# Attention with half-row second score passes, two parts of the product with v and both transposes per unit, in a written order

## The chip, the cores and the metric

One core of one Trainium2 chip runs the whole kernel. The metric is the device time of one execution in microseconds (us). The kernel's engines are TensorE (PE; PEld is its weight load), VectorE (DVE), ScalarE (ACT), GpSimd (POOL) and SyncE (SP), which issues most DMAs. SBUF is the on-chip memory, PSUM the eight banks that TensorE writes.

## The reference

One encoder layer on 2048 tokens of width 1024: an RMS norm, an input projection, differential attention beside a retention, an output projection, and a two-layer MLP with squared ReLU. The change concerns the attention. It has 4 heads; each has two components c of queries and keys of 64 features, and values of 128:

```
s = einsum('bhcqd,bhckd->bhcqk', q_blk, k) * dk ** -0.5
p = softmax(s - slope[h] * |qpos - kpos|, axis=-1)
a = p[:, :, 0] - lam[h] * p[:, :, 1]
out = einsum('bhqk,bhkd->bhqd', a, v)
```

## The kernel before, in words

All large products run in the type fp32r on operands that are split into a high and a low part, so that a product is three matmuls (high by high, high by low, low by high; `mm3`). The stages are: input projection (to about 661 us), retention, attention (about 775 to 1363 us), output projection, MLP.

A tile is 128 queries of one head: 4 heads by 16 tiles are 64 tiles, numbered i. Two tiles are a group (256 queries). Keys of a head lie in `ka` as 128 rows by 2 components by 2048 keys; for both components rows 0 to 63 hold the high parts of the 64 features and rows 64 to 127 the low parts. `qa` holds the high parts of the queries in both halves of its rows, `qb` the low parts in both halves. So one matmul of 128 rows with `qa` gives high by high plus high by low, and a second one with `qb` (the second pass) gives low by high plus low by low.

Steps of a tile, with their lines:

- `scores` (L992): a slot is one component and half of the keys (1024). Four matmuls of 512 columns fill two PSUM banks (L1011 with `qa`, L1012 with `qb`). VectorE reads both banks in one instruction, adds the bias, writes `p` and keeps a running minimum `nm` (L1016). After a component's second half ScalarE takes the exp of 128x2048 in place and sums it into `l` (L1028). Scores have two PSUM buffers of two banks (`ps_s`).
- `combine` (L1031): VectorE computes `ratio` = -lam * l0 / l1 (L1037, L1038) and `rl` = 1 / l0 (L1039); GpSimd computes p0 += ratio * p1 in two halves, a multiplication and an addition each (L1043, L1044).
- `turn` (L1197): four transposes of p0 through TensorE (L1205) into one PSUM bank `pa` (two buffers, `ps_t`); ScalarE copies the high part `aTh` (L55), VectorE subtracts to get the low part `aTl` (L56). Four turns cover a tile's 2048 keys.
- `weigh` (L1210): the product with v, for a group: a slot is two key blocks, 6 matmuls of 256 columns (L36, L37, L38) into `po`. After the eighth slot ScalarE copies `po` to `oT` (L1223).
- `turn_back` (L1226): two transposes of `oT` (L1231), scaling by `rl` on ScalarE (L1234), and a DMA to DRAM.

The loop over i from 2 to 63 has four slots. In each slot it writes, in this order, scores of tile i, one turn of tile i - 2, one weigh slot of tile i - 4, in slot 1 of an even tile a turn_back, and after slot 3 the combination of tile i. Only TensorE follows that written order (L1239); the order on VectorE, ScalarE, GpSimd and SyncE comes from a planner that places what it expects to be ready. Tiles 0 and 1 are scored earlier, in eight steps between those of the retention (`lead_scores`, L1049, with single banks), where TensorE, VectorE and ScalarE follow the written order. `load_group` (L962) brings queries by 4 DMAs a group, `load_keys` (L940) keys by 4 DMAs a head, `load_values` (L948) the values, and computes the next head's bias from the one before on VectorE (L958). After the loop the last turns and products are interleaved with the start of the output projection.

The `p` tiles have six places, two per tile, so tile i + 3 takes the places of tile i.

Of the kernel before, what the change touches and what calls it, by code (L numbers as in the profile page):

```python
# [17 lines left out]
P = 128  # L18
# [536 lines left out]
def encoder(ctx: ExitStack, tc: tile.TileContext, a: dict, out: bass.AP, dbg=None):  # L555
# [406 lines left out]
    def load_group(g):  # L962
        h, qs = g // (S // QG), g % (S // QG) * QG
        qa = kp_.tile([P, 2, QG], F32R, tag="qa", name="qa")
        qb = kp_.tile([P, 2, QG], F32R, tag="qb", name="qb")
        for t, s in ((qa, qh_d), (qb, ql_d)):
            for half in range(2):
                d = nc.sync.dma_start(
                    t[half * 64 : half * 64 + 64].bitcast(F32),
                    s[h][:, qs : qs + QG].rearrange("(c d) q -> d c q", d=64).bitcast(F32),  # L970
                )
        groups[g] = dict(loaded=d, q=(qa, qb), a=[None] * 4, rl=kp_.tile([P, 2], F32, tag="rl", name="rl", bufs=6), po=None)
# [19 lines left out]
    def scores(i, slot, banks):  # L992

        c, hf = divmod(slot, 2)
# [4 lines left out]
        if slot == 0:  # L999
            tiles[i] = dict(p=[], l=[])  # L1000
        if hf == 0:
            tiles[i]["p"].append(hp.next([P, S], F32, "p"))
            tiles[i]["nm"] = kp_.tile([P, 4], F32, tag="nm", name="nm", bufs=8)
        p, nm = tiles[i]["p"][c], tiles[i]["nm"]
        ql = slice(qi * P, qi * P + P)
        w = 1024 // len(banks)
        for b, sc in enumerate(banks):
# [5 lines left out]
            n = hf * len(banks) + b  # L1013
            k0 = hf * 1024 + b * w
            b0 = k0 + S - P - qt * P
# [10 lines left out]
        if hf == 1:  # L1026
            l = kp_.tile([P, 1], F32, tag="l", name="l", bufs=12)
            nc.scalar.activation(p[:], p[:], AF.Exp, bias=nm[:, n : n + 1], scale=-1.0, accum_out=l[:])  # L1028
            tiles[i]["l"].append(l)

    def combine(i):  # L1031
# [4 lines left out]
        ratio = kp_.tile([P, 1], F32, tag="ratio", name="ratio", bufs=6)  # L1036
        nc.vector.reciprocal(ratio[:], ls_[1][:])  # L1037
        nc.vector.tensor_scalar(ratio[:], ratio[:], ls_[0][:], nlam[:, h : h + 1], op0=ALU.mult, op1=ALU.mult)  # L1038
        nc.vector.reciprocal(groups[g]["rl"][:, qi : qi + 1], ls_[0][:])  # L1039
# [9 lines left out]
    def lead_scores(n):  # L1049
        i, slot = divmod(n, 4)  # L1050
        scores(i, slot, [ret.bank([P, 512], "sc") for _ in range(2)])
        if slot == 3:
            combine(i)
# [136 lines left out]
    with ExitStack() as ph:  # L1190
# [6 lines left out]
        def turn(i, k4):  # L1197
            g, qi = divmod(i, 2)
            p0 = tiles[i]["p"][0]
            if qi == 0:  # L1200
# [9 lines left out]
        def weigh(g, slot):  # L1210
# [10 lines left out]
            if slot == 7:  # L1221
                oT = ap2.tile([P, QG], F32, tag="oT", name="oT")
                nc.scalar.activation(oT[:], po[:], AF.Copy)  # L1223
                groups[g]["oT"] = oT
# [14 lines left out]
        ph.enter_context(tc.manual_schedule(engines={mybir.EngineType.PE}))  # L1239
        load_values(0)  # L1240
        for i in range(LT, NI):
            for slot in range(4):
# [14 lines left out]
                if 0 < j and j % 2 == 0 and slot == 1:  # L1257
                    turn_back(j // 2 - 1)
                if slot == 3 and LEAD <= i < NI - 1:
                    combine(i)  # L1260
# [18 lines left out]
        def ws(*slots):  # L1279
            for slot in slots:  # L1280
                weigh(g - 1 + slot // 8, slot % 8)

        places = (hp.next([P, 2, DM], F32R, "wo") for _ in range(6))
        parts = [norms(tt, eg[:, 2], eg[:, 2]) for tt in (0, 4)]
        turn(NI - 2, 0)
# [5 lines left out]
        ph.enter_context(tc.manual_schedule(engines=ENGINES))  # L1291
# [340 lines left out]
```

## Time and profile before

| | |
|---|---|
| median of 3 runs | 2812.51 us (2811.05 to 2817.38) |
| profiled execution | 2811.03 us, span 2809.2 us |
| mean granted TensorE clock | 0.984 of full speed |
| attention loop, tiles 4 to 63 | 819.0 to 1341.5 us |

A profile page gives per engine the busy time and its share of the span; the chain of waits follows the work that ended last backwards, from each instruction to what released it. A line names a line of the kernel; lines 36 to 38, 50, 55 and 56 are those of helpers that several stages use. Durations of matmuls are those of one pass through the pipeline; the step from one to the next is shorter and is seen in the chain, where each piece lasts until the next begins.

### The profile page before, as it was taken

The numbers are of one execution on the slowest core, as the hardware profiler recorded it, in microseconds if no ns is written. First come the engines' busy times: TensorE is split into PE (matmuls) and PEld (weight loads), VectorE is DVE, ScalarE is ACT, GpSimd is POOL, SyncE is SP. The second block draws the span as 40 slices with busy tenths as digits, with TensorE's granted clock in tenths as the row PEclk, the third lists the DMA queues.
The fourth block names the chain that finished last, engine by engine and source line by source line (L and its number), as shares of the span: only waits on it lengthen the run. The fifth ranks groups of instructions, "written<-read, shape, count | busy, mean of one in ns | idle before, by whom it ended". The sixth has DMA issues, their size and how long they took to land.

```text
span 2809.2 us, 41043 instructions
## 1 busy us (share of the span) xinstructions
PE 2711.6 (97%) x15488; PEld 2327.6 (83%) x15488; DVE 1902.3 (68%) x2887; ACT 1303.7 (46%) x1852; POOL 1317.3 (47%) x756
## 2 busy tenths in 40 slices
PE   6998999998889999999899999999999999999999
PEld 4898989997768888888787788888888888888887
DVE  7888864787779989999898465665556435435542
ACT  5344422344457777777543345544445332222221
POOL 4235322513358787888544367765565204323320
PEclk8999999999899999999999999999999999999999
DMA  3565683259523131321367777776445848755461
GB/s 128 178 198 173 222 296 113 91 171 265 136 76 91 50 88 53 84 97 55 133 213 237 274 226 253 235 276 234 157 143 188 291 161 311 274 189 174 159 246 45
DMA packets 356518, 490.31 MB, mean 175 GB/s; under 512 B 23008, under 2 KB 252896, under 8 KB 348384
## 3 DMA queue, kind: packets, MB, share of 16 engines
q1 hardware_dynamic: 334096, 462.52, 50.4%
q10 hardware_dynamic: 21648, 20.98, 2.2%
q0 software_dynamic: 576, 4.19, 0.4%
q8 instruction: 122, 2.00, 0.3%
q14 instruction: 76, 0.62, 0.1%
HBM read 313.55 MB, written 174.06 MB: 174 GB/s over the span
## 4 chain that ended last, share of the span: by engine, by line
PE 78%; DVE 7%; DMA 2%; issue 1%; POOL 1%; ACT 1%; SPq 0%; DVEq 0%; ACTq 0%; POOLq 0%
PE ps L38 10%; PE ps L36 10%; PE ps L37 10%; PE p L36 7%; PE p L38 7%; PE p L37 7%; PE pa L1205 4%; PE sc L1011 4%; PE sc L1012 4%; PE po L36 2%; PE po L38 2%; PE po L37 2%; PE mm L38 1%; PE mm L37 1%; PE mm L36 1%
## 5 line engine op out<-in xcount | busy, mean ns | idle before, releaser
L37 PE MATMUL p<-wl,ah 128*128 128x512 f32 x896 | 348.5, 389 | 0.0
L36 PE MATMUL p<-wh,ah 128*128 128x512 f32 x896 | 348.4, 389 | 0.0
L262 POOL TENSOR_TENSOR s<-raw 128x1024 f32<-128x1024 f32 x58 | 148.0, 2552 | 373.8 <-DMA raw<-in_w_in 109.7
L303 DVE TENSOR_TENSOR c<-ps,c 128x512 f32<-128x512 f32 x360 | 238.3, 684 | 116.4 <-PE ps L38 112.1
L50 DVE TENSOR_TENSOR wl<-s,wh 128x1024 fp32r<-128x1024 f32 x120 | 192.4, 1605 | 172.0 <-ACT wh L44 172.0
L44 ACT ACTIVATE ah<-ra 128x1024 fp32r<-128x1024 f32 x112 | 112.6, 1052 | 412.6 <-PE p L37 410.8
L1044 POOL TENSOR_TENSOR p<-p 128x1024 f32<-128x1024 f32 x127 | 303.2, 2410 | 0.1
L1028 ACT ACTIVATE p<-p,nm 128x2048 f32<-128x2048 f32 x128 | 256.9, 2007 | 36.4 <-DVE nm L1016 35.4
L50 DVE TENSOR_TENSOR ah<-ra,ah 128x1024 fp32r<-128x1024 f32 x76 | 103.7, 1399 | 218.4 <-ACT ah L44 218.4
L1455 POOL TENSOR_TENSOR c<-c 128x512 f32<-128x512 f32 x128 | 196.4, 1559 | 109.5 <-ACT c L1458 107.6
L38 PE MATMUL p<-wh,ah 128*128 128x512 f32 x608 | 236.5, 389 | 0.0
L1516 POOL TENSOR_TENSOR t<-br 128x1024 f32<-128x1024 f32 x32 | 77.1, 2411 | 336.3 <-DMA br<-in_w_mlp 173.1
L44 ACT ACTIVATE wh<-s 128x1024 fp32r<-128x1024 f32 x120 | 126.5, 1057 | 208.8 <-PE ps L37 108.3
L1011 PE MATMUL sc<-ka,qa 128*128 128x512 f32 x512 | 207.1, 404 | 3.3 <-ACT yt L544 2.8
L1043 POOL TENSOR_SCALAR p<-p,ratio 128x1024 f32<-128x1024 f32 x127 | 141.8, 1129 | 143.0 <-DVE ratio L1038 111.3
L1012 PE MATMUL sc<-ka,qb 128*128 128x512 f32 x512 | 202.5, 396 | 0.0
L36 PEld LDWEIGHTS p<-wh,ah 128*128 128x128 f32 x896 | 168.2, 188 | 34.9
L37 PEld LDWEIGHTS p<-wl,ah 128*128 128x128 f32 x896 | 168.2, 188 | 34.9
L55 ACT ACTIVATE aTh<-pa 128x512 fp32r<-128x512 f32 x256 | 151.0, 591 | 82.7 <-PE pa L1205 80.1
L1016 DVE CUSTOM_DVE_ANT_0 p<-sc,bias,nm 128x1024 f32<-128x1024 f32 (+1 forms) x136 | 167.7, 1233 | 22.5 <-PE sc L1012 20.8
L1205 PEld LDWEIGHTS pa<-ident,p 128*128 128x128 f32 x1024 | 120.5, 141 | 64.9 <-issue 30.7
L56 DVE TENSOR_TENSOR aTl<-pa,aTh 128x512 fp32r<-128x512 f32 x256 | 170.2, 685 | 4.5 <-DMA vh<-vhd 3.7
(371 smaller groups left out, 8110.7 us busy)
## 6 DMA issues: line engine op xcount, KB each, us to landing
br<-in_w_mlp SPq DMA_DIRECT2D x88, 512.0 KB, 5.6
raw<-in_w_mlp SPq DMA_DIRECT2D x32, 1024.0 KB, 6.0
raw<-in_w_in SPq DMA_DIRECT2D x28, 1024.0 KB, 5.9
xt<-in_x SPq DMA_DIRECT2D x20, 512.0 KB, 5.0
q<-rqd SPq DMA_DIRECT2D x16, 512.0 KB, 10.2
qa<-qhd SPq DMA_DIRECT2D x64, 128.0 KB, 3.0
qb<-qld SPq DMA_DIRECT2D x64, 128.0 KB, 3.0
ua11d<-c SPq DMA_DIRECT2D x32, 256.0 KB, 3.0
```

Of the source, the lines that this page charges most:

```text
L36: nc.tensor.matmul(out, ah, bh, start=first, stop=False)
L37: nc.tensor.matmul(out, ah, bl, start=False, stop=False)
L38: nc.tensor.matmul(out, al, bh, start=False, stop=last)
L44: nc.scalar.activation(hi, src, AF.Copy)
L50: e.tensor_tensor(out=lo, in0=src, in1=hi.bitcast(F32), op=ALU.subtract)
L303: nc.vector.tensor_tensor(out=o[:], in0=x0[:], in1=x1[:], op=op)
L1011: nc.tensor.matmul(sc[:, o : o + 512], qa[:, c, ql], r, start=True, stop=False)
L1012: nc.tensor.matmul(sc[:, o : o + 512], qb[:, c, ql], r, start=False, stop=True)
L1028: nc.scalar.activation(p[:], p[:], AF.Exp, bias=nm[:, n : n + 1], scale=-1.0, accum_out=l[:])
L1044: e.tensor_tensor(out=p0, in0=p0, in1=p1, op=ALU.add)
L1205: nc.tensor.transpose(pa[:, j], p0[:, kt * P : (kt + 1) * P], ident[:])
L1455: nc.gpsimd.tensor_tensor(out=u[n][:], in0=u[x0][:], in1=u[x1][:], op=op)
```

## The change

- `load_keys`: component 1 of `ka` is stored with its halves exchanged, high parts in rows 64 to 127, low parts in rows 0 to 63.
- `load_group`: `qb` holds the low parts of component 0 in rows 0 to 63 and of component 1 in rows 64 to 127 (one DMA in place of two).
- `scores` works on a unit: both components, and as many keys as a buffer holds (1024 in the loop, 512 in the lead). Full passes of 128 rows with `qa` come first, then half-row passes of 64 rows with `qb` against the high parts of the keys, the two components one behind the other; low by low is no longer computed. Two reductions on VectorE follow.
- `exps` and `inverse` are functions of their own; the multiplication of `ratio` moves from VectorE to GpSimd, `rl` from `combine` to `turn`, the copy `oT` from `weigh` to `away`.
- The loop: slot 0 and slot 2 hold a unit and a weigh slot, slots 1 and 3 a weigh slot and two turns of tile i - 2. The exp of component 1 comes in slot 3 of loop i, its inverse after the first unit of loop i + 1, the exp of component 0 and the combination in slot 1 of loop i + 1.
- In the loop all four engines TensorE, VectorE, ScalarE and GpSimd follow the written order, and so they do in the part behind it.

```diff
     def load_keys(h):
...
-            rs = slice(c * 64, c * 64 + 64)
-            d = nc.sync.dma_start(ka[0:64, c].bitcast(F32), kh_d[h][rs, :].bitcast(F32))
-            nc.sync.dma_start(ka[64:128, c].bitcast(F32), kl_d[h][rs, :].bitcast(F32))
+            rs, os = slice(c * 64, c * 64 + 64), slice(64 - c * 64, 128 - c * 64)
+            nc.sync.dma_start(ka[rs, c].bitcast(F32), kh_d[h][rs, :].bitcast(F32))
+            nc.sync.dma_start(ka[os, c].bitcast(F32), kl_d[h][rs, :].bitcast(F32))
...
     def load_group(g):
...
+        nc.sync.dma_start(qb[:, 0].bitcast(F32), ql_d[h][:, qs : qs + QG].bitcast(F32))
...
-    def scores(i, slot, banks):
+    def scores(i, n, banks):
...
+        w = banks[0].shape[1]
+        k0 = n * w
+        for c, sc in enumerate(banks):
             for o in range(0, w, 512):
-                k0 = hf * 1024 + b * w + o
-                r = ka[:, c, k0 : k0 + 512]
-                nc.tensor.matmul(sc[:, o : o + 512], qa[:, c, ql], r, start=True, stop=False)
-                nc.tensor.matmul(sc[:, o : o + 512], qb[:, c, ql], r, start=False, stop=True)
+                nc.tensor.matmul(sc[:, o : o + 512], qa[:, c, ql], ka[:, c, k0 + o : k0 + o + 512], start=True, stop=False)
+        for o in range(0, w, 512):
+            for c, sc in enumerate(banks):
+                rs = slice(c * 64, c * 64 + 64)
+                nc.tensor.matmul(sc[:, o : o + 512], qb[rs, 0, ql], ka[rs, c, k0 + o : k0 + o + 512], start=False, stop=True)
...
+    def exps(i, c):
+        l = kp_.tile([P, 1], F32, tag="l", name="l", bufs=12)
+        p, n = tiles[i]["p"][c], tiles[i]["n"]
+        nc.scalar.activation(p[:], p[:], AF.Exp, bias=tiles[i]["nm"][c][:, n : n + 1], scale=-1.0, accum_out=l[:])
+        tiles[i]["l"][c] = l
+    def inverse(i):
+        tiles[i]["r"] = kp_.tile([P, 1], F32, tag="ratio", name="ratio", bufs=6)
+        nc.vector.reciprocal(tiles[i]["r"][:], tiles[i]["l"][1][:])
...
-        nc.vector.tensor_scalar(ratio[:], ratio[:], ls_[0][:], nlam[:, h : h + 1], op0=ALU.mult, op1=ALU.mult)
-        nc.vector.reciprocal(groups[g]["rl"][:, qi : qi + 1], ls_[0][:])
+        nc.gpsimd.tensor_scalar(ratio[:], ratio[:], ls_[0][:], nlam[:, h : h + 1], op0=ALU.mult, op1=ALU.mult)
...
-        ph.enter_context(tc.manual_schedule(engines={mybir.EngineType.PE}))
+        ph.enter_context(tc.manual_schedule(engines=ENGINES | {mybir.EngineType.Pool}))
...
-                if i >= LEAD:
-                    scores(i, slot, [ps_s.tile([P, 1024], F32, tag="sc", name="sc")])
-                if 0 <= i - LT:
-                    turn(i - LT, slot)
+                if slot % 2 == 0:
+                    scores(i, slot // 2, [ps_s.tile([P, 1024], F32, tag="sc", name="sc") for _ in range(2)])
+                    if slot == 0 and i > LEAD:
+                        inverse(i - 1)
                 j = i - LV
+                if 0 < j and j % 2 == 0 and slot == 0:
+                    turn_back(j // 2 - 1)
                 if 0 <= j:
                     weigh(j // 2, j % 2 * 4 + slot)
...
+                if slot % 2 == 0:
+                    continue
+                if 0 <= j and j % 2 and slot == 3:
+                    away(j // 2)
+                turn(i - LT, slot - 1)
+                turn(i - LT, slot)
+                if slot == 3:
+                    exps(i, 1)
+                elif i > LEAD:
+                    exps(i - 1, 0)
+                    combine(i - 1)
...
         parts = [norms(tt, eg[:, 2], eg[:, 2]) for tt in (0, 4)]
+        exps(NI - 1, 0)
+        inverse(NI - 1)
         turn(NI - 2, 0)
         turn(NI - 2, 1)
```

## Rows read from the trace of the kernel before

**Rows 1.** The page, busy time, share of the span and instructions of each engine.
```profile
PE 2711.6 (97%) x15488; PEld 2327.6 (83%) x15488; DVE 1902.3 (68%) x2887; ACT 1303.7 (46%) x1852; POOL 1317.3 (47%) x756
```
**Rows 2.** Busy time by stretches: stretch and length, then each engine's.
```profile
799.00:819.00 20.00, 13.93 (x65) 10.40 (x66) 14.57 (x32) 12.63 (x18) 11.28 (x8) 0.91 0.48 138
819.00:1341.50 522.50, 519.75 (x3419) 444.85 (x3418) 472.73 (x904) 404.87 (x568) 419.73 (x242) 1.00 0.26 73
```
**Rows 3.** Chain of waits in the loop: start us, length us, what.
```profile
1003.36 0.23 PE sc L1011
1003.83 0.63 PE pa L1205 x4
1004.46 0.12 PE po L36
1006.11 0.44 PE pa L1205 x4
```
**Rows 4.** Waits in the loop, 830 to 1330 us: total, times, longest.
```profile
PEld pa L1205 <- issue: 23.1, 57, 0.4
```
**Rows 5.** Chain of waits where lead scores stand between the retention's steps.
```profile
780.74 0.23 PE sc L1012
780.97 1.09 PE rS L501 x16
782.06 0.58 PE rt L542 x4
783.80 0.43 PE sc L1011
785.96 0.43 PE sc L1011
```
**Rows 6.** TensorE in order of time: start us, us, what.
```profile
780.90 1.16 PE L501 MATMUL rS<-q,kT 64*128 64x128 f32 x16
781.99 0.65 PE L542 MATMUL rt<-ident,yT 128*128 128x128 f32 x4
```
**Rows 7.** The score tiles' instructions in the loop: duration ns min/median/max.
```profile
L1012 PEld LDWEIGHTS sc<-ka,qb x480: 187/188/192, 818.8 to 1339.9; 128*128 128x128 f32 x160
L1012 PE MATMUL sc<-ka,qb x480: 387/395/398, 819.1 to 1340.1; 128*128 128x512 f32 x160
```
**Rows 8.** Groups of VectorE instructions, 830 to 1330 us: busy us, mean ns.
```profile
L1038 DVE TENSOR_SCALAR ratio<-ratio,l,nlam 128x1 f32<-128x1 f32 x58 | 15.8, 273 | 2.1
L958 DVE TENSOR_SCALAR bias<-bias 128x3968 f16<-128x3968 f16 x2 | 2.6, 1294 | 0.0
```
**Rows 9.** Groups of GpSimd instructions, in the loop and of the whole span.
```profile
L1044 POOL TENSOR_TENSOR p<-p 128x1024 f32<-128x1024 f32 x116 | 276.4, 2406 | 0.0
L1043 POOL TENSOR_SCALAR p<-p,ratio 128x1024 f32<-128x1024 f32 x116 | 129.1, 1126 | 100.7 <-DVE ratio L1038 100.7
L661 POOL IOTA prow<- 128x1 f32 x1 | 0.1, 132 | 0.0
```
**Rows 10.** One tile in order of time: transposes to copy, exp to its sum.
```profile
1101.96 0.60 PE L1205 MATMUL pa<-ident,p 128*128 128x128 f32 x4
...
1102.60 0.60 ACT L55 ACTIVATE aTh<-pa 128x512 fp32r<-128x512 f32 x1 [0.79 <-PE pa L1205]
...
1104.05 2.01 ACT L1028 ACTIVATE p<-p,nm 128x2048 f32<-128x2048 f32 x1
...
1106.18 0.16 DVE L1039 RECIPROCAL rl<-l 128x1 f32<-128x1 f32 x1 [0.48 <-ACT p L1028]
```
**Rows 11.** TensorE after the last score pass.
```profile
1342.74 0.65 PE L1205 MATMUL pa<-ident,p 128*128 128x128 f32 x4 [0.64 <-DVE aTl L56]
```
**Rows 12.** GpSimd and VectorE after the loop, in order of time.
```profile
1345.39 1.61 POOL L1043 TENSOR_SCALAR p<-p,ratio 128x1024 f32<-128x1024 f32 x1 [2.23 <-DVE ratio L1038]
1347.08 3.23 POOL L1044 TENSOR_TENSOR p<-p 128x1024 f32<-128x1024 f32 x1
1349.30 1.05 DVE L1149 TENSOR_SCALAR mst<-mst 128x4 f32<-128x4 f32 x1
```

More of the change, by code (lines that the diff above doesn't have):

```diff
@@ L965, in load_group @@
         qb = kp_.tile([P, 2, QG], F32R, tag="qb", name="qb")
[L966 to L971, printed above, removed]
+        nc.sync.dma_start(qb[:, 0].bitcast(F32), ql_d[h][:, qs : qs + QG].bitcast(F32))
+        for half in range(2):
+            d = nc.sync.dma_start(
+                qa[half * 64 : half * 64 + 64].bitcast(F32),
+                qh_d[h][:, qs : qs + QG].rearrange("(c d) q -> d c q", d=64).bitcast(F32),
+            )
         groups[g] = dict(loaded=d, q=(qa, qb), a=[None] * 4, rl=kp_.tile([P, 2], F32, tag="rl", name="rl", bufs=6), po=None)
@@ L998, in scores @@
         qa, qb = groups[g]["q"]
[L999 to L1004, printed above, removed]
+        if n == 0:
+            tiles[i] = dict(
+                p=[hp.next([P, S], F32, "p") for _ in range(2)], l={},
+                nm=[kp_.tile([P, 4], F32, tag="nm", name="nm", bufs=8) for _ in range(2)],
+            )
         ql = slice(qi * P, qi * P + P)
-        w = 1024 // len(banks)
-        for b, sc in enumerate(banks):
+        w = banks[0].shape[1]
+        k0 = n * w
+        for c, sc in enumerate(banks):
             for o in range(0, w, 512):
-                k0 = hf * 1024 + b * w + o
-                r = ka[:, c, k0 : k0 + 512]
-                nc.tensor.matmul(sc[:, o : o + 512], qa[:, c, ql], r, start=True, stop=False)
-                nc.tensor.matmul(sc[:, o : o + 512], qb[:, c, ql], r, start=False, stop=True)
-            n = hf * len(banks) + b
-            k0 = hf * 1024 + b * w
-            b0 = k0 + S - P - qt * P
+                nc.tensor.matmul(sc[:, o : o + 512], qa[:, c, ql], ka[:, c, k0 + o : k0 + o + 512], start=True, stop=False)
[3 more added lines that the diff above has]
+                nc.tensor.matmul(sc[:, o : o + 512], qb[rs, 0, ql], ka[rs, c, k0 + o : k0 + o + 512], start=False, stop=True)
+        b0 = k0 + S - P - qt * P
+        for c, sc in enumerate(banks):
+            p, nm = tiles[i]["p"][c], tiles[i]["nm"][c]
             nc.vector.tensor_tensor_reduce(
@@ L1025, in scores @@
             )
[L1026 to L1029, printed above, removed]
+        tiles[i]["n"] = n
+    def exps(i, c):
[6 more added lines that the diff above has]
+        nc.vector.reciprocal(tiles[i]["r"][:], tiles[i]["l"][1][:])
     def combine(i):
@@ L1035, in combine @@
         ps_, ls_ = tiles[i]["p"], tiles[i]["l"]
-        ratio = kp_.tile([P, 1], F32, tag="ratio", name="ratio", bufs=6)
-        nc.vector.reciprocal(ratio[:], ls_[1][:])
-        nc.vector.tensor_scalar(ratio[:], ratio[:], ls_[0][:], nlam[:, h : h + 1], op0=ALU.mult, op1=ALU.mult)
-        nc.vector.reciprocal(groups[g]["rl"][:, qi : qi + 1], ls_[0][:])
+        ratio = tiles[i]["r"]
+        nc.gpsimd.tensor_scalar(ratio[:], ratio[:], ls_[0][:], nlam[:, h : h + 1], op0=ALU.mult, op1=ALU.mult)
         for k2 in range(2):
@@ L1049, in lead_scores @@
     def lead_scores(n):
-        i, slot = divmod(n, 4)
-        scores(i, slot, [ret.bank([P, 512], "sc") for _ in range(2)])
-        if slot == 3:
+        i, part = divmod(n, 4)
+        scores(i, part, [ret.bank([P, 512], "sc") for _ in range(2)])
+        if part == 3:
+            exps(i, 1)
+            inverse(i)
+            exps(i, 0)
             combine(i)
@@ L1199, in turn @@
             p0 = tiles[i]["p"][0]
+            if k4 == 0:
+                nc.vector.reciprocal(groups[g]["rl"][:, qi : qi + 1], tiles[i]["l"][0][:])
             if qi == 0:
@@ L1220, in weigh, with away @@
                 mm3(nc, po[:], vh[:, kt], vl[:, kt], th[:, j], tl[:, j], kt == 0, kt == NT - 1)
[L1221 to L1224, printed above, removed]
+        def away(g):
+            oT = ap2.tile([P, QG], F32, tag="oT", name="oT")
+            nc.scalar.activation(oT[:], groups[g]["po"][:], AF.Copy)
+            groups[g]["oT"] = oT
         def turn_back(g):
@@ L1249, in encoder @@
                     load_group(i // 2)
[L1250 to L1253 removed]
+                if slot % 2 == 0:
+                    scores(i, slot // 2, [ps_s.tile([P, 1024], F32, tag="sc", name="sc") for _ in range(2)])
+                    if slot == 0 and i > LEAD:
+                        inverse(i - 1)
                 j = i - LV
+                if 0 < j and j % 2 == 0 and slot == 0:
+                    turn_back(j // 2 - 1)
                 if 0 <= j:
                     weigh(j // 2, j % 2 * 4 + slot)
[L1257 to L1260, printed above, removed]
+                if slot % 2 == 0:
[5 more added lines that the diff above has]
+                if slot == 3:
+                    exps(i, 1)
+                elif i > LEAD:
+                    exps(i - 1, 0)
+                    combine(i - 1)
             if i == NI - 4:
@@ L1281, in ws @@
                 weigh(g - 1 + slot // 8, slot % 8)
+                if slot % 8 == 7:
+                    away(g - 1 + slot // 8)
         places = (hp.next([P, 2, DM], F32R, "wo") for _ in range(6))
         parts = [norms(tt, eg[:, 2], eg[:, 2]) for tt in (0, 4)]
+        exps(NI - 1, 0)
+        inverse(NI - 1)
         turn(NI - 2, 0)
```

2 lines of the change are left out of this document (removed).

## The prediction

> **What bounds the kernel now.** I read the busy shares first, then the busy time by stretches, then the chain of waits, then who waits for whom. TensorE is busy for 97% of the span, VectorE for 68% [rows 1]; but shares are means over stages, so the stretches decide. Only the attention loop and its two ends are touched. From 819.0 to 1341.5 us the loop runs its 60 full tiles (4 to 63): 522.5 us, 8.71 us each, and there TensorE is busy 99.5%, VectorE 90%, GpSimd 80%, ScalarE 77% [rows 2]. Divided by 60: VectorE 7.88, GpSimd 7.00, ScalarE 6.75 us a tile. So TensorE is the bound, and the next engine is only 0.8 us behind it.
>
> The chain of waits there holds TensorE alone [rows 3]: a score pass of 512 columns steps on by 0.23 us, a pass of the product with v by 0.12, four transposes by 0.44. A tile has 16 score passes (3.73), 24 product passes (2.86), 16 transposes (1.76) and every second tile two more for the result (0.11): 8.46 us. The other 0.25 is waiting; it shows where four transposes take 0.63 instead of 0.44 [rows 3], behind the slot of the transposes' own bank (the rows give "issue", 23.1 us in 57 times [rows 4]).
>
> **The change on TensorE.** Each score unit (1024 keys, both components) had 8 full passes; it now has 4 full ones and 4 half-row ones, in two pairs, rows 0 to 63 beside rows 64 to 127. Do two halves share a step? The loop shows none, but the retention stage has such pairs: 16 passes of 64 rows and 128 columns take 1.09 us in the chain [rows 5], and from the first start to the rows' next form 1.09 again (780.90 to 781.99 [rows 6]). Alone, transposes of 128 columns step by 0.11, so 16 in a row would be 1.76. They do run in pairs. I take one score step per pair, 0.24; both bounds follow from the same rows: 0.23 (free partner) and 0.47 (no sharing).
>
> But the same rows show what it costs to go into and out of such a form. Eight pairs at 0.11 are 0.88; 1.09 is 0.21 more: the way in. On the way out, the four transposes behind them take 0.58 against the 0.44 of a group that comes straight after score passes, 0.14 more; and a full score pass straight behind half-form passes of the retention takes 0.43, twice (783.80 and 785.96), against 0.23: 0.20 more [rows 3, 5]. In and out together 0.35 to 0.41; I take 0.38. A unit goes in and out once, a tile twice: 0.76 us. The bounds: nothing (a 512-column pass, longer than the retention's, might cover the weight load; the 0.43 of a full score pass speaks against that, and no crossing in the rows is free), and 0.70 per round trip, if both crossings expose what a pass lasts beyond its step (395 - 233 ns) and a whole weight load (188 ns) [rows 7]. I stay with 0.38, since it comes from score passes themselves.
>
> Sum for TensorE: 8 full passes 1.87, 4 pairs 0.96, product 2.86, transposes 1.87 with the result's, crossings 0.76: 8.32 us against 8.46. So the halves save 0.91 and the crossings take 0.76 back.
>
> The Trainium skill has two sentences on this. TensorEngine Tiling (Array Packing), Theoretical Speedup, gives up to 2x where the contraction is 64 or less; by that alone the tile would lose 0.91 us. The same page, Key Properties, says that changing the tiling mode drains the engine; by that and the rows above it loses 0.14. The trace agrees with the second sentence (0.35 to 0.41 us a round trip), and with the first only inside a run of pairs.
>
> **The change in the order.** Transposes now come eight together, with product passes before them, and both score banks are written in one unit. What is late next, per engine, for a tile of about 8.4 us:
> - VectorE: 7.88 less the ratio's multiplication (0.27 [rows 8]), which goes to GpSimd: 7.6. The unit's second half of banks is read by the time it is wanted: from the end of a unit the two reductions take 2 x 1.2 us, and TensorE is then 12 product passes, 8 transposes and two full passes further on, 1.43 + 0.88 + 0.47 + 0.2 = 3.0.
> - ScalarE: 6.75, the same work.
> - GpSimd: 7.00 plus one small multiplication on 128x1. No row has it; VectorE's takes 0.27, GpSimd's own 128x1 iota 0.13 [rows 8, 9]. I take 0.2: 7.2.
> - A ring that did not bind before. The second exp of a tile (its component 0) now stands on ScalarE behind two copies of the tile before, these behind their transposes, these behind the combination on GpSimd, and the next combination behind that exp. Round it: first transpose to copy 0.64 (1101.96 to 1102.60), two copies 1.18, exp until its sum is there 2.13 (1104.05 to 1106.18) [rows 10], ratio 0.2, multiplication 1.13, addition of the first half 2.41 [rows 9], handshakes some 0.05: 7.74 us. Under 8.32, so it is covered, by 0.6.
>
> The waits of today (0.25) come from VectorE's splits that hold the transposes' two banks; with eight transposes once per half tile and slack on every engine most of that goes. I leave 0.08. Tile: 8.40; saved 0.31 x 60 = 18.6 us.
>
> **The ends.** (1) After tile 63 no score unit stands before the first transposes of tile 62, so the ring shows: in the loop the unit, its crossing out and 12 product passes (3.2 us) cover it; without them TensorE waits 3.2 - 0.6 = 2.6 us, where it waits 0.64 now [rows 11]: 2 us lost. (2) Three biases of later heads, 1.29 us each on VectorE [rows 8], now stand at fixed places right before the first reduction of a head. Behind each are queued two reductions, and score banks behind these; some 0.8 us of it is slack: 0.5 x 3 = 1.5 us. (3) In the lead-in both exps of a tile now come after its last quarter, 2 us later for the first; the loop's first tiles wait for other things there anyway (TensorE busy 13.9 of 20 us [rows 2]): 1 us, either sign. DMAs: a group brings 3 instead of 4, keys 4 as before, none of them among the loop's waits, of which the largest on TensorE is that of [rows 4]: nothing; without that cover a group's transfer could only come earlier, there is one less. Ends: 4.5 us lost.
>
> On (2), the Trainium skill, SBUF — State Buffer, section SBUF: two separate sides, says that VectorE in some modes and GpSimd lock each other out of a shared port for a whole instruction. A row agrees: 128x4 elements took VectorE 1.05 us and ended as GpSimd's addition did [rows 12]. By that rule a bias that meets an addition would wait up to 2.41 us more, 7 us in all, and the sum would be some 7 us later; the two biases in the loop stood where GpSimd rested.
>
> Sum: 18.6 - 4.5 = 14 us less. The profiled execution took 2811.0 us (its span is 2809.2, 1.8 us lie around it), the median of the runs is 2812.5: forecast 2798.
>
> **The rivals.**
> - *Crossings are hidden* under 512-column passes. Then TensorE needs 7.56, and the ring (7.74) is the bound; with 0.1 of waits 7.85, saved 0.86 x 60 = 52, the ends cost 6 because the ring has no slack: 2767. For it: long passes give a weight load more room. Against: the 0.43.
> - *Crossings cost more* (the slower side): place, the edges of each half-row run, four per tile; price 0.70 a round trip instead of 0.38. Tile 8.40 + 0.64 = 9.04, lost 0.33 x 60 = 20 plus 4.5: 2837. It decides from (8.71 - 8.40 + 0.76 - 0.08 for the ends) / 2 = 0.50 us a round trip on: there the loop's gain only pays for the ends. Against: no row over 0.21 a crossing.
> - *The ring binds*: GpSimd's two instructions at the 1.61 and 3.23 us of the last tile, when VectorE worked on the same kind [rows 12], give a ring of 9.0 and 2836. Against: in the loop VectorE reads banks beside it, then as now.
> - *The halves do not pair up* at this type (the pairs in the rows are of another): four more steps of 0.23, tile 9.3, 2853.
> - *Fixed order*: today's planner lets VectorE and ScalarE take what is ready; waits in line eat the 0.31: 2806 to 2818.
>
> **How the numbers follow.** Forecast 0.50 (own range 2788 to 2808), hidden 0.15, dear 0.15, ring 0.08, order 0.06, no pairs 0.06. A measurement here can tell 0.2%, 5.6 us, from no change. Faster: 0.45 + 0.15 + 0.05 from partial forms of the dear and the ordered case, 0.65; same 0.13; slower 0.22. The range takes in the hidden case and the dear bound up to 2834 and leaves out the pairless case and the tops of ring and dear, under 0.2.
>
> **What would show it.** In the profile after: pairs of half passes that start within some 10 ns of each other and step by 0.24; the full pass or product pass at either edge 0.1 to 0.2 us longer than its step, 0.76 a tile in sum; loop tiles of 8.4 us; TensorE still the bound, with VectorE at 7.6 of 8.4; a wait of 2 to 3 us for GpSimd's addition after the last score unit. A tile near 7.8 with TensorE waiting for GpSimd says that crossings are free; over 8.7 with TensorE full, that they are dear; over 8.7 with gaps, ring or order. Outside the stretch 775 to 1400 us nothing should change.

## The result, and the profile after

The changed kernel takes 2793.22 us (median of 4 runs, 2790.52 to 2793.75) against 2811.78 us (4 runs, 2810.68 to 2817.38): ratio 0.9932, 95% interval 0.9921 to 0.9944, 18.6 us less. The forecast was 2798, its own range 2788 to 2808. The profiled execution took 2790.5 us, its span 2788.7.

Busy shares of the page, in answer to [rows 1]; TensorE is still the bound. Its weight loads cover less time, not because a load of 64 rows is shorter (186 ns in the median against 188), but because the two loads of a pair run at the same time (they begin 3 to 4 ns apart, as at 1005.32):

```profile
PE 2693.0 (97%) x15488; PEld 2281.1 (82%) x15488; DVE 1884.8 (68%) x2823; ACT 1293.3 (46%) x1852; POOL 1353.8 (49%) x820
```

Busy time by stretches after the change (PE, PEld, DVE, ACT, POOL, then granted clock, DMA share, GB/s): from the first score pass to tile 4, the 60 full tiles, and the part from there to the output projection's first pass. The second line answers to the second of [rows 2]:

```profile
775.41:811.45 36.04, 30.33 (x210) 18.66 (x209) 24.85 (x60) 20.16 (x27) 15.90 (x12) 0.98 0.37 102
811.45:1315.55 504.10, 499.44 (x3418) 399.37 (x3418) 462.60 (x844) 393.95 (x568) 444.50 (x300) 1.00 0.25 68
1315.55:1340.32 24.77, 19.37 (x146) 18.05 (x143) 18.86 (x34) 18.04 (x30) 17.16 (x10) 0.93 0.04 12
```

The 60 tiles take 504.1 us where they took 522.5: 8.40 each instead of 8.71. That this is the forecast's number to the hundredth is luck: two sizes were off and cancelled (see below). By the same three stretches the trace before had 39.2, 522.5 and 21.7 us (first score pass at 779.77, the output projection's first pass at 1363.17). So the change took 3.2 us off the lead-in and 18.4 off the tiles and put 3.1 on the end: 18.5 of the 20.5 us between the two spans. (Tile 4's first pass came at 818.74 before; counted from there, 0.3 us move from the lead-in to the tiles.) The other 2 us lie in stages with the same code: the retention's first pass (L460) came at 636.07 before and 632.38 now, and between 631 and 637 in all fourteen traces of this study, so this is the spread of single executions.

The chain of waits in a unit (start, length, what), in answer to [rows 3]: no piece is late, the eight transposes take 0.87 where four took 0.63, and the product's first pass takes 0.32 behind half-row passes instead of 0.12 (the last row is the next unit's transposes):

```profile
1003.59 0.87 PE pa L1218 x8
1004.47 0.93 PE sc L1009 x4
1005.39 0.66 PE sc L1014 x4
1006.06 0.32 PE po L36
1006.38 0.12 PE po L37
...
1007.69 0.87 PE pa L1218 x8
```

The two passes of a pair begin 2 to 4 ns apart, as the prediction said of its first sign; in this row of TensorE up to 1005.33 both of the first pair have begun:

```profile
1005.32 0.50 PE L1014 MATMUL sc<-ka,qb 64*128 64x512 f32 x2
```

The second sign, a step of 0.24, does not show inside a unit: its second pair begins 0.34 us behind the first. In a longer run (**twice** below) the pairs begin 0.34, 0.57 and 0.80 us behind the first: a step of 0.23 from the second on, so the 0.1 belongs to the way in.

The waits in the loop (830 to 1310 us), TensorE's, its weight loads' and GpSimd's. The wait of the transposes' weight loads in [rows 4], 23.1 us in 57 times, is gone. The two rows of PEld are the edges of the half-row runs: before the first half-row load, and before the first full load behind them, the loads stand still for 0.36 us and wait for nothing that the profile shows.

```profile
POOL ratio L1047 <- ACT p L1033: 41.1, 54, 3.8
PEld sc L1014 <- issue: 40.8, 112, 0.4
PEld po L36 <- issue: 31.4, 86, 0.5
...
PE sc L1009 <- DVE nm L1018: 4.2, 6, 1.0
```

All of TensorE's 4.2 us lie at the three changes of head. VectorE's and GpSimd's rows there, in order of time, then TensorE's:

```profile
912.87 2.36 DVE L959 TENSOR_SCALAR bias<-bias 128x3968 f16<-128x3968 f16 x1
915.40 1.23 DVE L1018 CUSTOM_DVE_ANT_0 p<-sc,bias 128x1024 f32<-128x1024 f32 x1 [0.17 <-PE pa L1218]
```

```profile
911.78 2.40 POOL L1052 TENSOR_TENSOR p<-p 128x1024 f32<-128x1024 f32 x1
914.16 2.05 POOL L1051 TENSOR_SCALAR p<-p,ratio 128x1024 f32<-128x1024 f32 x1
```

```profile
916.69 0.73 PE L1009 MATMUL sc<-ka,qa 128*128 128x512 f32 x2 [0.98 <-DVE nm L1018]
917.84 0.73 PE L1009 MATMUL sc<-ka,qa 128*128 128x512 f32 x2 [0.41 <-DVE nm L1018]
```

The bias, 1.29 us in [rows 8], takes 2.36, and GpSimd's multiplication next to it 2.05 instead of 1.13 [rows 9]. The bias ends at 915.23, 1.05 us behind the end of the addition (914.18) that was running when it began. This holds in every trace where a bias met an instruction of GpSimd: it ended 1.05 us behind it, whether it had begun 0.16 us (**ratiodve**), 0.84 (**twice**), 1.23 (**full2**) or 1.31 (here) ahead of that end. In the trace before it had begun 0.25 ahead, so the 1.29 of [rows 8] holds some of this already; with GpSimd at rest (790.92) a bias took 1.19. Units are read from the start of one's scores to the start of the next one's: 4.09, 4.10, 4.09 and 4.26 (with a turn_back) in turn, 8.27 a tile; at a head two of them take 5.50 and 4.81. At the middle head the second one took 6.28, and there the granted clock had fallen after TensorE's waits, to 0.50 from 1053.2 to 1056.5, its lower level of 1.2 GHz (this row's last column but two takes in some time at the upper level):

```profile
1054.00:1057.00 3.00, 3.00 (x18) 3.00 (x18) 2.19 (x4) 0.00 (x0) 2.92 (x3) 0.57 0.00 0
```

Three heads cost 1.95 + 3.4 + 1.95 = 7.3 us. A second trace of the same kernel (**after2**) had 4.80 in that place, and 5.8 in all. Besides, the first unit of tile 4 takes 4.87, 0.8 us more than the later ones, in both traces.

The first transposes behind the loop, in answer to [rows 11], wait 2.73 us for GpSimd (forecast 2.6); the product passes behind them step by 0.21 instead of 0.12 until 1322.7, with the clock at its lower level again (granted 0.50 from 1319.4 to 1322.8):

```profile
1318.52 1.18 PE L1218 MATMUL pa<-ident,p 128*128 128x128 f32 x8 [2.73 <-POOL p L1052]
```

### The profile page after: what moved, and what is told of

It reads as the page before. It is cut to its first block, busy times and chain, and to the rows that moved or that the text cites. A ratio compares the mean times of both kernels' runs of the same rounds, so it can differ in the third digit from the quotient of the medians.

```text
span 2788.7 us, 41023 instructions
## 1 busy us (share of the span) xinstructions
PE 2693.0 (97%) x15488; PEld 2281.1 (82%) x15488; DVE 1884.8 (68%) x2823; ACT 1293.3 (46%) x1852; POOL 1353.8 (49%) x820
## 4 chain that ended last, share of the span: by engine, by line
PE 81%; DVE 10%; issue 3%; DMA 3%; ACT 2%; POOL 1%; SPq 1%; ACTq 0%; DVEq 0%; POOLq 0%
PE ps L36 11%; PE ps L38 11%; PE ps L37 11%; PE p L37 7%; PE p L38 7%; PE p L36 7%; PE sc L1009 4%; PE pa L1218 4%; PE sc L1014 3%; PE po L36 3%; PE po L38 2%; PE po L37 2%; PE mm L37 1%; PE mm L36 1%; PE mm L38 1%
## 5 line engine op out<-in xcount | busy, mean ns | idle before, releaser
L36 PE MATMUL p<-wh,ah 128*128 128x512 f32 x896 | 348.4, 389 | 0.0
L36 PEld LDWEIGHTS p<-wh,ah 128*128 128x128 f32 x896 | 168.2, 188 | 34.9
L55 ACT ACTIVATE aTh<-pa 128x512 fp32r<-128x512 f32 x256 | 139.3, 595 | 96.3 <-PE pa L1218 94.7
L1009 PE MATMUL sc<-ka,qa 128*128 128x512 f32 x512 | 153.9, 419 | 9.2 <-DVE nm L1018 9.2
L1018 DVE CUSTOM_DVE_ANT_0 p<-sc,bias 128x1024 f32<-128x1024 f32 (+1 forms) x128 | 149.5, 1205 | 17.6 <-PE sc L1014 17.1
L50 DVE TENSOR_TENSOR wl<-raw,wh 128x1024 fp32r<-128x1024 f32 x89 | 142.5, 1602 | 24.4 <-ACT wh L44 24.4
L36 PE MATMUL po<-aTh,vh 128*128 128x256 f32 x512 | 158.3, 309 | 0.0
```

The lines of the kernel that those rows point to most:

```text
L36: nc.tensor.matmul(out, ah, bh, start=first, stop=False)
L50: e.tensor_tensor(out=lo, in0=src, in1=hi.bitcast(F32), op=ALU.subtract)
L1009: nc.tensor.matmul(sc[:, o : o + 512], qa[:, c, ql], ka[:, c, k0 + o : k0 + o + 512], start=True, stop=False)
L1018: nc.vector.tensor_tensor_reduce(out=p[:, k0 : k0 + w], in0=sc[:], in1=bias[:, b0 : b0 + w], scale=1.0, scalar=nm[:, n - 1 : n] if n else ...
```

## The experiments

Kernels of one group ran on one chip, with the kernel before beside them. The theory under test: half rows save two steps of four per unit and give most of it back at the edges; the order saves the old waits; the bias takes some back.

### Half rows or order

**full2**: second passes of 128 rows again (for them the low parts of the queries are brought into both halves of `qb`, as before), order kept.

```diff
-                rs = slice(c * 64, c * 64 + 64)
-                nc.tensor.matmul(sc[:, o : o + 512], qb[rs, 0, ql], ka[rs, c, k0 + o : k0 + o + 512], start=False, stop=True)
+                nc.tensor.matmul(sc[:, o : o + 512], qb[:, c, ql], ka[:, c, k0 + o : k0 + o + 512], start=False, stop=True)
...
```

> Order and all of the changed kernel, but the second passes are again full passes of 128 rows with the low parts of the queries (low by low is computed again). Theory (a unit gains four steps of 0.23 us and gives most of it back where it goes into and out of the half-row form, 0.38 us a round trip): a unit takes 8 x 0.233 = 1.86 us against about 1.77 now, so a tile is 0.15 to 0.2 us longer, the loop 9 to 11 us, in all 2802 to 2805; and the order alone, without half rows, still brings some 8 to 10 of the 18.6 us. Rival A (crossings are free, the gain comes from the halves alone): a tile is 0.91 longer, 2848. Rival B (the halves bring nothing, all of the gain is the order's): the same time within 3 us, 2790 to 2796.

2800.59 us (before 2811.49; ratio 0.9966, 0.9953 to 0.9979). Its chain in the loop:

```profile
1008.27 0.93 PE sc L1009 x4
1009.20 0.92 PE sc L1013 x4
1010.12 0.12 PE po L36
```

Units take 4.17 three times and 4.41 in the first and third head, 8.46 a tile, just the 8.46 that the prediction had worked out for TensorE without waits (in the second and fourth head 4.15 and 4.38, 8.41; why, no run shows). Between the heads the loop before took 8.81 and 8.52 in turn, 8.66 on average. So there the order alone brings 0.20 to 0.25 us a tile, and the half rows 8.46 - 8.27 = 0.19 (0.14 in the other two heads). Two pairs in place of four passes save 0.466 a unit and the unit is 0.08 shorter (0.15 with a turn_back): the round trip costs 0.39 (0.32). Medians: about 11 us from the order, 7 to 8 from the half rows. The theory held, with 1.4 us less than its range of 2802 to 2805, and both rivals fell.

**twice**: each half-row pass issued twice in one run (the low-by-high term is counted twice).

```diff
-        for o in range(0, w, 512):
...
+        for rep in range(2):
+            for o in range(0, w, 512):
+                for c, sc in enumerate(banks):
...
+                        sc[:, o : o + 512], qb[rs, 0, ql], ka[rs, c, k0 + o : k0 + o + 512], start=False, stop=rep == 1
...
```

> The changed kernel, but every half-row pass is issued twice in the same run of half-row passes (the low-by-high term is counted twice): four pairs in a row per unit instead of two, and still one way in and one way out. It tells the price of a pair from the price of the crossing. Theory A (a pair takes one score step, 0.233 us, and the crossing is 0.385 a round trip): 0.47 us a unit more, 0.94 a tile, loop tiles of 9.2, about 58 us in all. Theory B (a pair takes 0.333 us, as the second pair of a unit does now, and the crossing only 0.285): 0.67 a unit, 1.33 a tile, tiles of 9.6, about 82 us in all.

One run: 2852.32 us. Its chain:

```profile
1008.27 1.12 PE sc L1015 x8
1009.39 0.32 PE po L36
```

Four pairs take 1.12 where two took 0.66: 0.23 a pair, units 4.55 to 4.57 and 4.73. That is theory A: a pair takes one score step, the rest is the crossing. Without sharing, four more passes would have added 0.93 a unit, not 0.46.

**tworuns**: the same passes, but full, half, full, half.

```diff
-        for c, sc in enumerate(banks):
-            for o in range(0, w, 512):
+        for o in range(0, w, 512):
+            for c, sc in enumerate(banks):
                 nc.tensor.matmul(sc[:, o : o + 512], qa[:, c, ql], ka[:, c, k0 + o : k0 + o + 512], start=True, stop=False)
-
-        for o in range(0, w, 512):
             for c, sc in enumerate(banks):
...
```

> The changed kernel, but a unit does one block of 512 keys after the other: two full passes, one half-row pair, two full passes, one half-row pair. The same passes, but two runs of half-row passes a unit instead of one. Theory A (0.385 us a round trip, a pair 0.233): 0.385 a unit more, 0.77 a tile, tiles of 9.04, about 48 us in all. Theory B (a pair 0.333 and the round trip 0.285): the second run saves the 0.10 by which the second pair is late now, so 0.185 to 0.285 a unit, tiles of 8.64 to 8.84, 23 to 35 us in all. Rival (crossings cost nothing, the longer steps at the edges are only how the records show them): no change.

One run: 2853.16 us, more than A's 48 us over the changed kernel. Its chain:

```profile
1008.31 0.47 PE sc L1009 x2
1008.77 0.43 PE sc L1012 x2
1009.20 0.66 PE sc L1009 x2
1009.87 0.42 PE sc L1012 x2
1010.29 0.32 PE po L36
```

From 1008.31 to the end of that L36 are 2.30 us, in the changed kernel 1.91 (1004.47 to 1006.38): the second round trip costs 0.39, as the first. The rest is a wait: three of four units have another 0.1 in front of their scores, since both components' banks are now complete only at the unit's end and VectorE is behind ("PEld sc L1009" waits for "DVE nm L1016" 54 times, 11.3 us, from 900 to 1300). Theory A holds for the price; its total was too low by that wait.

**bycomp**: two half-row passes on one half, then two on the other.

```diff
-        for o in range(0, w, 512):
-            for c, sc in enumerate(banks):
-                rs = slice(c * 64, c * 64 + 64)
+        for c, sc in enumerate(banks):
+            rs = slice(c * 64, c * 64 + 64)
+            for o in range(0, w, 512):
```

> The changed kernel, but the four half-row passes of a unit are issued component by component (two on rows 0 to 63, then two on rows 64 to 127) instead of in turns. Theory (two half-row passes share a step only if they follow each other on different rows): the middle two share one, the outer two have one each, three steps instead of two, 0.23 to 0.33 a unit, tiles of 8.73 to 8.93, 29 to 41 us in all. Rival A (no two pass side by side, the small gap in the records is not work done side by side): the same time as the changed kernel, since four passes take what they take in any order. Rival B (each of the row halves has a queue of its own): also no change, because both halves then always have work.

One run: 2794.13 us; units 4.08 to 4.12 and 4.26, as in the changed kernel. The expectation failed: the passes need not alternate. Rival A falls by **twice**. Rival B is what the trace shows: here too two passes have begun within 10 ns of each other,

```profile
1001.45 0.50 PE L1014 MATMUL sc<-ka,qb 64*128 64x512 f32 x2
```

and the other two begin 0.34 us later. These later two carry the signals that VectorE waits for, which stand on the last pass of each component. So the first passes of both components ran side by side, and the pass written third began ahead of the one written second: each half works off its own passes. A run of four can't show how far ahead it may look.

### The written order

**planned**: in the loop only TensorE in written order. In this run and the next, VectorE's and ScalarE's written order begins again behind the loop, ahead of tile 62's third quarter.

```diff
-        ph.enter_context(tc.manual_schedule(engines=ENGINES | {mybir.EngineType.Pool}))
+        ph.enter_context(tc.manual_schedule(engines={mybir.EngineType.PE}))
...
+        ph.enter_context(tc.manual_schedule(engines=ENGINES))
         turn(NI - 2, 2)
...
```

> The changed kernel, but in the loop only TensorE follows the written order; VectorE, ScalarE, GpSimd and SyncE get theirs from the planner again, as before the change. Theory (the written order takes away the 0.25 us of waits a tile because the eight transposes stand together once per half tile, not because the other engines are in written order; it costs at the three changes of head, where the bias stands in front of the first reductions): the tiles between take 8.27 as now, the stalls at the heads shrink from about 7 us to 2 or less, 2786 to 2793. Rival A (the written order on the other engines is what took the waits away): 0.1 to 0.25 us of waits a tile come back, 2800 to 2808. Rival B (the planner's combination comes later and the ring binds): tiles of 8.6 and more, above 2810.

2838.22 us, ratio 1.0097 (1.0081 to 1.0112). The theory fell, and rival A's price was far too low. The time lies where rival B put it, but TensorE doesn't wait for the ring here. TensorE's wait in the loop (830 to 1300 us), then ScalarE's rows around one:

```profile
PE pa L1218 <- ACT ot L1248: 27.7, 26, 1.3
```

```profile
1013.18 2.00 ACT L1033 ACTIVATE p<-p,nm 128x2048 f32<-128x2048 f32 x1
...
1015.18 1.99 ACT L1033 ACTIVATE p<-p,nm 128x2048 f32<-128x2048 f32 x1
...
1017.16 0.61 ACT L1248 ACTIVATE ot<-pz,rl 128x128 f32<-128x128 f32 x2
```

The planner put both exps of a tile ahead of the two scalings that free the bank of the result; of four units one took 5.83 instead of 4.26, and another 4.34 instead of 4.09.

**actorder**: ScalarE in written order too, VectorE, GpSimd and SyncE planned.

```diff
-        ph.enter_context(tc.manual_schedule(engines=ENGINES | {mybir.EngineType.Pool}))
+        ph.enter_context(tc.manual_schedule(engines={mybir.EngineType.PE, mybir.EngineType.Activation}))
...
```

> The changed kernel with TensorE and ScalarE in written order in the loop, and VectorE, GpSimd and SyncE in the planner's. With the planner on all three, ScalarE did both exps of a tile in one piece ahead of the two copies that free a bank (4.1 us), and TensorE waited 1.3 us every second tile, tiles of 9.15. Theory (ScalarE's order alone is what must be written): tiles of 8.27 to 8.4, about 2790 to 2800. Rival (VectorE's or GpSimd's order in the planner's hands is as bad): tiles over 8.6, above 2810.

One run: 2825.56 us, tiles of 8.93: the rival held. The wait (TensorE's in the loop, 830 to 1300 us), and GpSimd's rows of one tile:

```profile
PE pa L1218 <- POOL p L1052: 24.0, 52, 0.9
```

```profile
1008.30 0.33 POOL L1047 TENSOR_SCALAR ratio<-ratio,l,nlam 128x1 f32<-128x1 f32 x1 [1.58 <-ACT p L1033]
1008.73 2.22 POOL L1051 TENSOR_SCALAR p<-p,ratio 128x1024 f32<-128x1024 f32 x2
1010.92 2.39 POOL L1052 TENSOR_TENSOR p<-p 128x1024 f32<-128x1024 f32 x1
```

GpSimd did both multiplications and then both additions, so the first half is ready 1.1 us later, and the ring that the prediction drew now binds: 8.93 - 1.11 = 7.82 us without that, against 7.74 worked out.

**ratiodve**: the ratio's multiplication on VectorE, at the same place.

```diff
-        nc.gpsimd.tensor_scalar(ratio[:], ratio[:], ls_[0][:], nlam[:, h : h + 1], op0=ALU.mult, op1=ALU.mult)
+        nc.vector.tensor_scalar(ratio[:], ratio[:], ls_[0][:], nlam[:, h : h + 1], op0=ALU.mult, op1=ALU.mult)
```

> The changed kernel, but the multiplication of the ratio is back on VectorE, at the same place in the written order. Theory (in a written order VectorE must stand there until the second exp has its sum, 1.2 us behind the splits, and the next unit's reductions, which TensorE wants within some 0.6 us of when they are done, stand behind it): reductions 1.3 to 1.4 us later, TensorE waits 0.7 to 1.0 us a tile, loop tiles of 9.0 to 9.3, 2835 to 2855; the move to GpSimd is what lets the order be written. Rival (the prediction's own account of this edit: 0.27 us of VectorE's time, which has room, and a shorter ring): the same time within 2 us.

2856.91 us, ratio 1.0156 (1.0141 to 1.0171); the changed kernel beside it, **after2**, 2792.31 (ratio 0.9929, 0.9917 to 0.9942).

> The changed kernel as it is, once more, as the measure for the three beside it on the same chip: 2790 to 2796.

VectorE's rows; it stood 1.18 us for the exp, and the reduction of the second line stood behind it:

```profile
1008.42 0.27 DVE L1047 TENSOR_SCALAR ratio<-ratio,l,nlam 128x1 f32<-128x1 f32 x1 [1.18 <-ACT p L1033]
1008.61 1.27 DVE L1018 CUSTOM_DVE_ANT_0 p<-sc,bias,nm 128x1024 f32<-128x1024 f32 x1
```

A 0.27 us instruction costs 64.6 us: some 1.15 us of VectorE's time goes in each tile, and tiles take 9.42. The theory held, a little above its range of 2835 to 2855.

### The ends

**biasact**: the next head's bias by ScalarE, in quarters behind the exps of tiles 8 to 11 of the head before; **biaseven** the same in tiles 6, 8, 10 and 12.

```diff
-            nc.vector.tensor_scalar(bias[:], heads[h - 1]["bias"][:], SLOPES[h] / SLOPES[h - 1], None, op0=ALU.mult)
+        nc.scalar.activation(biases[h][:, cs], heads[h - 1]["bias"][:, cs], AF.Copy, scale=SLOPES[h] / SLOPES[h - 1])
...
                     exps(i, 1)
+                    if i < NI - NT and 8 <= i % NT < 12:
+                        bias_part(i // NT + 1, i % NT - 8)
```

> The changed kernel, but the next head's bias is computed by ScalarE in four quarters, in tiles 8 to 11 of the head before, instead of by VectorE at the change of head. Theory (VectorE's bias instruction of 128x3968 and GpSimd's additions hold each other up, 2.35 us instead of 1.29, and TensorE then waits for the first reductions and runs below full clock for some microseconds): the stalls at tiles 16, 32 and 48, about 7 us together, go; ScalarE has 1.5 us a tile free, so the quarters cost nothing: 2785 to 2788. Rival A (the stalls at the heads come from the keys' or the values' transfers or from GpSimd's instruction being slow of itself there): no change, 2791 to 2795. Rival B (the quarters of some 0.9 us delay the copies behind them): the stalls move to tiles 8 to 11, four times 0.3 to 0.6 a head, 2790 to 2796.

2791.32 us (ratio 0.9931, 0.9915 to 0.9948). The theory holds for its first half and rival B for the second: the stalls at the heads are gone (units 4.26 and 4.09 there), but two quarters a head cost 0.55 each:

```profile
886.71 1.03 ACT L980 ACTIVATE bias<-bias 128x992 f16<-128x992 f16 x1
887.63 0.63 ACT L1253 ACTIVATE ot<-pz,rl 128x128 f32<-128x128 f32 x2
```

The quarter stands ahead of the scalings, as the exp did in **planned**. Hence biaseven:

> The bias on ScalarE in quarters as before, but in tiles 6, 8, 10 and 12 of the head before, so that no quarter stands ahead of the two scalings of a result, which came 1.03 us late in tiles 9 and 11 and held TensorE up by 0.55 us each. Theory (the stalls of the changes of head are the bias, those of the quarters are only their place): 1.1 us a head more are saved, 3.3 us, in all some 7 us less than the changed kernel, 2785 to 2789. Rival (ScalarE has no room for a quarter anywhere, since its second exp stands in the ring): 0.5 us at each of the twelve quarters, 2790 to 2794.

2783.91 us (ratio 0.9898, 0.9883 to 0.9912), against 2792.31 beside it. The theory held: behind the first unit of tile 4 no unit of the loop is late, and TensorE has no idle time from 820 to 1300 us:

```profile
820.00:1300.00 480.00, 480.00 (x3313) 385.60 (x3311) 440.73 (x816) 393.48 (x564) 427.45 (x291) 1.00 0.26 70
```

This version beats both kernels. From the first score pass to the projection's first pass it takes 556.9 us, the second trace of the changed kernel 563.6: 6.7 of the 8.4 us between the medians.

**tail**: behind the loop four product slots ahead of tile 62's transposes, that tile's second half on VectorE.

```diff
-            e = nc.vector if k2 == 0 and i == NI - 1 else nc.gpsimd
+            e = nc.vector if (i, k2) in ((NI - 1, 0), (NI - 2, 1)) else nc.gpsimd
...
+        combine(NI - 2, (1,))
+        ws(0, 1, 2, 3)
         turn(NI - 2, 0)
         turn(NI - 2, 1)
-        ws(0, 1)
         turn_back(g - 2)
...
```

> The changed kernel, but behind the loop four product slots stand before the first transposes of tile 62 instead of behind them, and the second half of that tile's combination is done by VectorE behind the loop instead of by GpSimd. Theory (the 2.73 us that TensorE waits there for GpSimd are the ring shown bare, and any TensorE work that is ready covers them): the output projection starts about 3 us earlier, 2789 to 2791. Rival A (the work moved up is missing later, when tile 63's combination is late): the wait only moves by a few microseconds, 2792 to 2795. Rival B (VectorE and GpSimd hold each other up where both combine): 2794 to 2798.

2793.82 us (ratio 0.9938, 0.9919 to 0.9956): rival A held. The wait of 2.73 us is gone, and another stands some 3 us further on, at the first transpose of the result:

```profile
1325.55 0.44 PE L1246 MATMUL pz<-ident,oT 128*128 128x128 f32 x2 [2.04 <-DVE aTl L56]
```

From the last score pass to the projection it took 28.0 us, the changed kernel 27.4.

**best2**: biaseven, with all eight ready product slots ahead of the last tiles' work and VectorE on two second halves.

```diff
+            e = nc.vector if k2 == 1 and i >= NI - 2 else nc.gpsimd
...
+        combine(NI - 2, (1,))
...
+        ws(0, 1, 2, 3)
+        turn_back(g - 2)
         turn(NI - 2, 0)
         turn(NI - 2, 1)
...
+        ws(4, 5)
+        turn(NI - 2, 2)
+        turn(NI - 2, 3)
         combine(NI - 1)
...
+        ws(6, 7)
...
```

> The quarters of the bias in tiles 6, 8, 10 and 12, and behind the loop another order: tile 62's second half and tile 63's second half are combined by VectorE, all eight product slots that don't need tiles 62 and 63 stand ahead of what does, and the norms of the next stage come later on VectorE. Theory (the 24.8 us between the loop and the output projection hold 17.6 us of TensorE work, and the rest is order): 2 to 4 us less than with the bias alone, 2782 to 2786. Rival (the ring and the splits of the last two tiles set the end whatever stands beside them): the same as with the bias alone, within 1.5 us.

This kernel also leaves out the last step of the first norms ahead of the output projection (two multiplications on VectorE, two on GpSimd). 2785.02 us (ratio 0.9903, 0.9887 to 0.9919): even with that step left out nothing is gained over biaseven. The rival held: 557.3 us from first score pass to projection against 556.9. What bounds that end is not settled. TensorE's longest waits in it are 2.3 and 1.7 us for ScalarE's copy of a result and its scalings, and 1.6 for a split of VectorE's.

## Why the prediction was right, and where only its sum was

**The crossing: right, with some luck.** 0.38 a round trip, with the 0.43 of a lead score pass [rows 5] as its best witness; 0.39 from full2 and again from tworuns. But the passes in front of those score passes have 128 rows and 64 columns, another half form:

```profile
784.86 1.09 PE L517 MATMUL ry<-sd,v 128*64 128x128 f32 x16
```

The only way out of half-row passes in the rows was 0.14, by transposes. That a longer pass loses 0.2 behind half-row passes too (0.32 instead of 0.12) only the trace after showed. A pair 0.24; measured 0.23. The halves' net gain of 0.14 a tile is 0.14 to 0.19. What the Trainium skill's TensorEngine Tiling (Array Packing), Theoretical Speedup, gives, up to 2x, the trace shows only for a pair by itself (0.23 for two passes); a unit with its edges gains 0.08 of 0.47.

**Waits and heads: two sizes off that cancelled, by luck.** The prediction left 0.08 us of waits in a tile; between heads there are none, and the rest of the sum came out 0.05 lower (8.27 against 8.32). That is 0.13 x 60 = 8 us better. Three biases were priced at 1.5 us and cost 7.3 in this trace, 5.8 in another: 4 to 6 worse. The first unit of tile 4, 0.8 us late, had no term. The slack behind a bias was counted, but the bias at 1.29 us; it takes 2.36, since all but a little of it comes behind GpSimd's addition, and GpSimd's next instruction grows by 0.9. That the two biases of the loop before "stood where GpSimd rested" is not quite so: each began while an addition had 0.23 to 0.25 us to go, and they too ended 1.05 us behind it. The rule that the prediction set beside it (the Trainium skill, SBUF — State Buffer, SBUF: two separate sides), with 7 us, was the better price, and the trace agrees with it: bias and additions ran one behind the other. That the stalls are the bias's is shown: without it on VectorE they are gone.

**The ratio's multiplication: the step that failed.** "7.88 less the ratio's multiplication (0.27 [rows 8]), which goes to GpSimd: 7.6" booked a load, where the point was a wait: 64.6 us. The sum wasn't hurt, because the edit was made. On GpSimd it takes 0.34 and not 0.2.

**The order: right in size, wrong in why.** "With eight transposes once per half tile and slack on every engine most of that goes": the waits went, but the 0.25 took in the changes of head and the first unit of tile 4; between heads it was 0.20. And the slack on the engines doesn't suffice. With the same transposes and the other engines planned, the kernel is 27 us slower than before. The rival "Fixed order" had it the wrong way round: the written order is what this arrangement lives on, though the wait in line that the rival names is what ratiodve shows. The ring was right: 7.74 against 7.82 in actorder. In the changed kernel one exp of component 0 follows the other by 8.19 us (1000.95 to 1009.14), with 0.33 us to spare between the end of the first half's addition (1007.20) and its transposes (1007.53): 7.86.

**The ends.** Tail 3.1 us (forecast 2): 2.73 of wait less the 0.64 of before, and then product passes at half clock (twelve that step by 0.21 instead of 0.12: about 1.1). Lead-in 3.2 us better (forecast 1, either sign, and taken as a loss in the sum). It lies in tiles 2 and 3, which took 19.1 us and take 15.4 (16.3 in the second trace, where the granted clock was 0.50 for some 3.4 us of them, as before the change). Before the change, TensorE stood there 2.4, 1.3 and 1.0 us for VectorE's splits, first here:

```profile
807.64 0.63 PE L1205 MATMUL pa<-ident,p 128*128 128x128 f32 x4 [2.43 <-DVE aTl L56]
```

Those waits are gone; shorter ones for VectorE's reductions, 0.35 to 0.64 us each, stand in their place. full2 has 15.2 there, so the half rows have no part in it.

In sum some 18 us by these terms instead of 14: 8 more from the tiles and 4 from the lead-in, 6 less at the heads, 1 less at the tail and 1 at the first unit of tile 4. So the forecast of 2798 came within 5 us of 2793 in part because terms of 4 to 8 us cancelled.

## What to carry to other kernels

Price a half-row form by its edges: here a round trip of 0.39 us stands against 0.23 saved per pair, so it pays from two pairs in a run on, and every further pair in the same run is gain. Before an instruction is moved between engines, look at what it waits for: in a written order everything behind it waits too, and 0.27 us can cost a microsecond per tile. A long VectorE instruction beside a busy GpSimd is to be put on an engine that has room, at a place with nothing urgent behind it: that alone brought 8.4 us more.

## What was not expected of the hardware

- The half-row passes of one row half need not alternate with those of the other: two and two took as long as one and one (units 4.07 to 4.12 in both), and the pass written third began before the one written second.
- A round trip is about as dear with one pair in the run as with two, 0.39 us. Where two transposes of the result follow instead of the product it is 0.32; why, no run shows.
- After waits of 0.97 and 0.41 us TensorE ran 3.3 us at a granted clock of 0.50 in one trace, and after 0.99 and 0.41 it stayed at 1.00 in another of the same kernel; so one stall cost 1.95 us or 3.4.
- A bias of 128x3968 on VectorE that began beside a GpSimd addition ended 1.05 us behind that addition whenever it had begun, and GpSimd's next instruction took about as much longer (2.05 instead of 1.13).
